# LN1 of a transformer trunk in groups of four channel tiles, with its element-wise work on VectorE

## The chip, the cores and the metric

The kernel runs on one core of one Trainium2 chip. The metric is the device time of one execution in microseconds (us). TensorE, VectorE, ScalarE, GpSimd and SyncE have an instruction queue each, in the fixed order in which the program was written; semaphores order them among each other. In the rows they are PE (PEld is its weight load), DVE, ACT, POOL and SP.

## The reference

One encoder layer works on 576 tokens of 2048 channels (512 of a prompt, 64 of a sample). The change lies between the mixer's last projection and the first product of the feed-forward network:

```python
x = layer_norm(DN_ALPHA * x + g1 * mix, ln1_g, ln1_b)      # mix = m @ w_out
u = ln_plain(x) * (1 + sc2) + sh2
f = (jax.nn.silu(u @ w_gate) * (u @ w_up)) @ w_down
x = layer_norm(DN_ALPHA * x + g2 * f, ln2_g, ln2_b)
```

Each normalization needs mean and variance over the 2048 channels of a token, and the second, parameter-free one (LN0) works on what the first (LN1) gives. Everything is fp32. The vectors sc2, sh2 and g1 differ between prompt and sample.

## The kernel before

Activations lie channel-major: 16 tiles of 128 channels (partitions) by 576 tokens. The tokens are worked in two halves, hf = 0 with 320 and hf = 1 with 256. An fp32 product is made of three matmuls: weights and activations are both split into a high and a low part (hi, lo and xh, xl), and each step of 128 input channels (a **tick**) does hi by xh, hi by xl and lo by xh (`mm_steps`, L312 to L316; in the last stage below, L1351). ScalarE makes hi of a weight block of 128 by 1024 (L215), VectorE makes lo (L220); a block serves 8 ticks. There are four pairs of hi and lo, so that the blocks of the next 24 ticks can be ready ahead of TensorE (`take`, `advance`).

The four stages that the prediction speaks of follow each other on TensorE:

- **A**: the projection with `w_out` for hf 0, 256 ticks of 320 columns. Beside it the other engines run the chain of LN1 and LN0 for hf 1.
- **B**: gate and up projection for hf 1, eight tiles of 32 ticks of 256 columns (`gate_up(ft, 1)`). Beside it runs the chain for hf 0.
- **C**: the same for hf 0, 256 ticks of 320 columns. Beside it `combo` makes sums and differences of the activation blocks, which the next stage multiplies.
- **D**: the first hidden tile (ft 8) of the rest of gate and up, which are done by seven products of 24 matmuls of 288 columns each, in the order 2, 4, 3, 5, 1, 6, 7. Products 6 and 7 read the differences SD and SE, which are made while the first five run.

What runs beside TensorE is set by the list `fill.bg`. At each tick the list earns a credit, `fill.rate`, and its first step is issued when the credit covers the step's cost; a step of kind "pe" waits until 16 ticks have passed since the last other step. Since every queue is in order, the list sets where a step stands between the weight splits.

The chain (`ln_chain`, L1050) has 18 steps for each of three passes, one tile of 128 channels by 320 or 256 tokens in a step:

- `center`: VectorE subtracts the mean (L1078), ScalarE squares (L1080), GpSimd adds the squares up (L1071). A matmul with a matrix of 1/2048 (L1061) sums over the partitions and spreads the result to all of them; `newton_rsqrt` (L334) makes rstd at full width, with Ln and Exp on ScalarE.
- `affine`: VectorE multiplies by gain and rstd (L1087), ScalarE adds the bias (L1090) and squares (L1091), GpSimd adds the squares up and VectorE the values (L1071).
- `modulate`: VectorE subtracts the mean (L1105) and multiplies by scale and rstd (L1107), ScalarE adds the shift and writes xh (L1112), VectorE makes xl (L1120), and ScalarE keeps the residual (L1114), which a DMA stores (L1117). While these steps head the list, GpSimd makes lo of the weight blocks (L219).

A `combo` has five steps for 4 tiles, 128 by 1152: a on GpSimd (L1187), b and c on VectorE (L1190, L1195, L1197), d on ScalarE (L1201), e on VectorE (L1205). For SE, b is on GpSimd too.

Of the kernel before, what the change touches and what calls it, by code (L numbers as in the profile page):

```python
# [14 lines left out]
P = 128  # L15
# [22 lines left out]
def tile_trunk(ctx, tc, x_prompt, x_sample, c_prompt, c_sample, cache_k, cache_v, state_pool,  # L38
# [43 lines left out]
    def f(ap):  # L82
        return ap.bitcast(F32)
# [59 lines left out]
    class Weights:  # L143
# [59 lines left out]
        def advance(self, late=False):  # L203
            if self.nu < len(self.units):
                i = self.nu
                self.nu += 1
                a, b, _ = self.units[i]
                raw = self.view(a) if b is None else self.sum_of.pop(i)
                if i in self.direct:
                    self.ready.append((raw, a))  # L210
                    return
                kk, n = raw.shape[1], raw.shape[1] * raw.shape[2]
                hi, lo = (split3(t[:, :n], kk) for t in self.pairs[self.np % len(self.pairs)])
                self.np += 1
                nc.scalar.activation(hi, raw, AF.Copy)  # L215
                self.combine(i + 1)

                def low():
                    eng = nc.gpsimd if fill.bg and fill.bg[0][0] == "mod" else self.engs[i % len(self.engs)]  # L219
                    (eng or nc.vector).tensor_tensor(lo, raw, f(hi), op=OP.subtract)  # L220
                    if b is None:
                        self.release(a)

                if late:
                    fill.at(3, low)
                else:
                    low()
                self.ready.append((hi, lo))
# [15 lines left out]
    class Fill:  # L244
# [779 lines left out]

    cv = Carve(misc)
    axb = [cv(640), cv(640)]
    cv.o = 1920
    SR = [cv(320), cv(256)]
    s1_t = cv(320)
    cv.o = 1280  # L1030
    nwt = [cv(320), cv(320)]
    lt = Carve(region("late", [P, 2048]))
    s2_t, rs_t, sqt = lt(320), lt(320), [lt(320), lt(320)] + nwt

    def load_ax(hf, j2):
        n = HS[hf]
# [10 lines left out]
    def res(hf, j):  # L1047
        return R0[:, j, :] if hf == 0 else R1[j // 8][:, j % 8, :]

    def ln_chain(hf):  # L1050
        n = HS[hf]
        cost = 0.6 if hf else 1.15
        s1, s2, rs = s1_t[:, 0:n], s2_t[:, 0:n], rs_t[:, 0:n]
        mean, var = AT[0][:, 0:n], AT[1][:, 0:n]
        nw = [t[:, 0:n] for t in nwt]
        steps = []

        def pe(*pairs):
            def go():
                for src, dst in pairs:  # L1060
                    nc.tensor.matmul(dst, ones, src, start=True, stop=True)  # L1061
            steps.append(("pe", 0, go))

        def st(cost, f, kind="v"):
            steps.append((kind, cost, f))

        def acc(eng, s, j, t):
            if j == 0:
                eng.tensor_copy(s, t)
            else:  # L1070
                eng.tensor_tensor(s, s, t, op=OP.add)  # L1071

        def sq(j):
            return sqt[j % 4][:, 0:n]

        def center(j):
            if j < 16:
                nc.vector.tensor_tensor(res(hf, j), res(hf, j), mean, op=OP.subtract)  # L1078
            if 0 <= j - 1 < 16:
                nc.scalar.activation(sq(j - 1), res(hf, j - 1), AF.Square)  # L1080
            if 0 <= j - 2:
                acc(nc.gpsimd, s2, j - 2, sq(j - 2))

        def affine(j):
            if j < 16:
                x = res(hf, j)
                nc.vector.scalar_tensor_tensor(x, x, vt2[:, 16 + j:17 + j], rs, op0=OP.mult, op1=OP.mult)  # L1087
            if 0 <= j - 1 < 16:
                x = res(hf, j - 1)
                nc.scalar.activation(x, x, AF.Identity, bias=vt2[:, 31 + j:32 + j])  # L1090
                nc.scalar.activation(sq(j - 1), x, AF.Square)  # L1091
            if 0 <= j - 2:
                acc(nc.gpsimd, s2, j - 2, sq(j - 2))
                acc(nc.vector, s1, j - 2, res(hf, j - 2))

        def rstd2():
            t = sqt[0][:, 0:n]
            nc.scalar.activation(t, mean, AF.Square)
            nc.vector.tensor_tensor(t, var, t, op=OP.subtract)
            newton_rsqrt(rs, t, n, nw)  # L1100

        def modulate(j):
            if j < 16:
                t = sq(j)
                nc.vector.tensor_tensor(t, res(hf, j), mean, op=OP.subtract)  # L1105
                for a, e, v in SEG[hf]:
                    nc.vector.scalar_tensor_tensor(t[:, a:e], t[:, a:e], modv("sc2", j, v), rs[:, a:e],  # L1107
                                                   op0=OP.mult, op1=OP.mult)
            if 0 <= j - 1 < 16:
                x = res(hf, j - 1)  # L1110
                for a, e, v in SEG[hf]:
                    nc.scalar.activation(xh(hf, j - 1)[:, a:e], sq(j - 1)[:, a:e], AF.Identity,  # L1112
                                         bias=modv("sh2", j - 1, v))
                nc.scalar.activation(x, x, AF.Identity, bias=mb[:, 1:2], scale=ALPHA)  # L1114
                if j % 4 == 0:
                    src = R0[:, j - 4:j, :] if hf == 0 else R1[(j - 4) // 8][:, (j - 4) % 8:(j - 4) % 8 + 4, :]
                    nc.gpsimd.dma_start(RESD[hf][:, j - 4:j, :], src)  # L1117
            if 0 <= j - 2:
                for a, e, v in SEG[hf]:
                    nc.vector.scalar_tensor_tensor(xl(hf, j - 2)[:, a:e], sq(j - 2)[:, a:e], modv("sh2", j - 2, v),  # L1120
                                                   f(xh(hf, j - 2)[:, a:e]), op0=OP.add, op1=OP.subtract)

        pe((SR[hf], mean))
        for j in range(18):
            st(cost, lambda j=j: center(j))
        pe((s2, var))
        st(2.0, lambda: newton_rsqrt(rs, var, n, nw))
        for j in range(18):
            st(cost, lambda j=j: affine(j))
        pe((s1, mean), (s2, var))  # L1130
        st(2.5, rstd2)
        for j in range(18):
            st(cost, lambda j=j: modulate(j), "mod")
        return steps

    for hf in (1, 0):
        n = HS[hf]
        for j in range(16):
# [5 lines left out]
            for jj in (j - 1, j):  # L1144
# [6 lines left out]
                if jj == 0:  # L1151
                    nc.vector.tensor_copy(SR[hf], x)
                else:
                    nc.vector.tensor_tensor(SR[hf], SR[hf], x, op=OP.add)
            nx = (1 - hf) * 8 + j // 2 + 2
            if nx < 16:
                load_ax(1 - nx // 8, nx % 8)
# [24 lines left out]
    def combo(x, y, op, dst, k, t, neg=False, eng=nc.vector):  # L1182

        t3 = split3(t[:, 0:1152], 4)

        def a():
            nc.gpsimd.tensor_tensor(t3, x(k, 4, 0)[0][2], y(k, 4, 0)[0][2], op=op)  # L1187

        def b():
            eng.tensor_tensor(t3, t3, f(x(k, 4, 1)[0][2]), op=OP.add)  # L1190

        def c():
            v = f(y(k, 4, 1)[0][2])
# [55 lines left out]
    for i, st in enumerate(todo):  # L1249
        a, b, c, d, e = st  # L1250
        if i == 0:
            chain.append((0.3, a))
        chain.append((1.2, b))
        if i:
            chain.append((1.2, todo[i - 1][4]))
            if i + 1 < len(todo):
                chain.append((0.3, todo[i + 1][0]))
            else:
                chain.append((0.3, SD[0][0]))
        elif len(todo) > 1:  # L1260
# [326 lines left out]
```

## Time and profile before

| | us |
|---|---|
| median of three runs (lowest, highest) | 3023.73 (3021.2, 3024.65) |
| the profiled execution | 3023.36 |
| its span, first to last instruction | 3021.6 |
| busy: PE, PEld | 2940.7 (97%), 2894.0 (96%) |
| busy: DVE, ACT, POOL | 2158.1 (71%), 1108.7 (37%), 494.1 (16%) |
| mean granted TensorE clock | 0.988 of full speed |

Busy time is the sum of an engine's instructions; the duration of an instruction is longer than its distance from the next where the two overlap. The page divides the span into 40 slices. TensorE's digit is 9 in 35 of them, 8 in the 1st, 18th and 22nd and 7 in the 20th and 40th; the granted clock is 7 tenths in the 20th, 8 in the 40th and 9 in the others. The 17th to the 22nd slice hold the four stages.

### The profile page before, as it was taken

What the parts mean: (1) busy time and instruction counts of PE and PEld (TensorE: products, weight loads), DVE (VectorE), ACT (ScalarE), POOL (GpSimd) and SP (SyncE); (2) the same over time, 40 slices, a digit from 0 to 9 for tenths busy, and PEclk for the clock granted to TensorE, in tenths of its full rate; (3) what the DMA queues carried; (4) which work ended last, traced back from release to release, by engine and by line L of the source; (5) the groups of instructions that cost most, each with busy time, mean ns of one, the idle gap of its engine ahead of it and who ended that gap; (6) DMA issues with size and microseconds to landing.
All of it is one profiled execution on the core that took longest, in us unless ns stands there. A gap on an engine that the chain in (4) does not pass through costs nothing. (4 is left out here: it accounts for less than half of the span.)

```text
span 3021.6 us, 52534 instructions
## 1 busy us (share of the span) xinstructions
PE 2940.7 (97%) x21675; PEld 2894.0 (96%) x21675; DVE 2158.1 (71%) x3310; ACT 1108.7 (37%) x1512; POOL 494.1 (16%) x504
## 2 busy tenths in 40 slices
PE   8999999999999999989798999999999999999997
PEld 7999999999999999989698999999999999999997
DVE  6777676898878757697887877777777753333467
ACT  4533333332222224465533434343433432122333
POOL 0023222113223220344432000000000010000001
PEclk9999999999999999999799999999999999999998
DMA  9864544675555446646453344343343473233444
GB/s 304 279 215 143 150 137 142 202 226 173 155 165 167 137 138 195 176 150 175 144 161 96 100 115 109 96 122 102 100 123 96 124 258 116 92 103 115 154 160 147
DMA packets 636015, 458.13 MB, mean 152 GB/s; under 512 B 17215, under 2 KB 619807, under 8 KB 634430
## 3 DMA queue, kind: packets, MB, share of 16 engines
q1 hardware_dynamic: 621136, 406.38, 45.7%
q0 software_dynamic: 14336, 48.24, 4.5%
q8 instruction: 169, 2.77, 0.4%
q14 instruction: 72, 0.59, 0.1%
q10 hardware_dynamic: 302, 0.15, 0.0%
HBM read 422.66 MB, written 32.04 MB: 150 GB/s over the span
## 5 line engine op out<-in xcount | busy, mean ns | idle before, releaser
L215 ACT ACTIVATE hi<-raw 128x1024 fp32r<-128x1024 f32 x689 | 724.5, 1057 | 1118.8 <-PE bank L314 341.9
L220 DVE TENSOR_TENSOR lo<-raw,hi 128x1024 fp32r<-128x1024 f32 x677 | 841.8, 1246 | 406.5 <-ACT hi L215 399.3
L316 PE MATMUL mm<-xh,lo 128*128 128x320 f32 (+1 forms) x2912 | 712.0, 297 | 23.4 <-DVE lo L220 13.3
L312 PE MATMUL mm<-xh,hi 128*128 128x320 f32 (+1 forms) x2912 | 727.7, 302 | 0.8 <-ACT hi L215 0.8
L314 PE MATMUL mm<-xl,hi 128*128 128x320 f32 (+1 forms) x2912 | 710.5, 296 | 7.9 <-DVE xl L1120 7.9
L316 PEld LDWEIGHTS mm<-xh,lo 128*128 128x128 f32 x2912 | 486.0, 190 | 27.0 <-DVE lo L220 15.8
L312 PEld LDWEIGHTS mm<-xh,hi 128*128 128x128 f32 x2912 | 490.1, 190 | 10.5 <-issue 4.0
L314 PEld LDWEIGHTS mm<-xl,hi 128*128 128x128 f32 x2912 | 486.9, 190 | 13.1 <-DVE xl L1120 12.6
L370 DVE SCALAR_TENSOR_TENSOR late<-raw,csil,late 128x256 f32<-128x256 f32 x960 | 418.7, 495 | 8.7 <-DMA raw<-in_w_ada_dram 8.6
L1351 PE MATMUL bank<-xh,hi 128*128 128x288 f32 x1152 | 341.3, 296 | 3.5 <-ACT xh L1201 3.5
L1351 PE MATMUL bank<-xl,hi 128*128 128x288 f32 x1152 | 341.2, 296 | 1.6 <-DVE xl L1205 1.6
L1351 PE MATMUL bank<-xh,lo 128*128 128x288 f32 x1152 | 341.0, 296 | 1.6 <-DVE lo L220 1.6
L312 PE MATMUL bank<-xh,hi 128*128 128x320 f32 (+1 forms) x1280 | 315.5, 295 | 2.2 <-DVE misc L1307 2.2
L316 PE MATMUL bank<-xh,lo 128*128 128x320 f32 (+1 forms) x1280 | 315.1, 295 | 1.6 <-DVE lo L220 1.6
L314 PE MATMUL bank<-xl,hi 128*128 128x320 f32 (+1 forms) x1280 | 314.4, 295 | 0.0
L1351 PEld LDWEIGHTS bank<-xh,hi 128*128 128x128 f32 x1152 | 216.8, 188 | 3.7 <-ACT xh L1201 3.7
L1351 PEld LDWEIGHTS bank<-xl,hi 128*128 128x128 f32 x1152 | 216.7, 188 | 2.2 <-DVE xl L1205 2.2
L1351 PEld LDWEIGHTS bank<-xh,lo 128*128 128x128 f32 x1152 | 216.8, 188 | 1.9 <-DVE lo L220 1.9
L312 PEld LDWEIGHTS bank<-xh,hi 128*128 128x128 f32 x1280 | 214.3, 188 | 2.5 <-DVE misc L1307 2.5
L316 PEld LDWEIGHTS bank<-xh,lo 128*128 128x128 f32 x1280 | 214.2, 188 | 1.8 <-DVE lo L220 1.8
L314 PEld LDWEIGHTS bank<-xl,hi 128*128 128x128 f32 x1280 | 213.4, 189 | 0.0
L375 POOL PARTITION_ALL_REDUCE late<-late x32 | 118.4, 3699 | 288.6 <-DVE late L370 244.2
(404 smaller groups left out, 4161.9 us busy)
## 6 DMA issues: line engine op xcount, KB each, us to landing
raw<-in_w_ada_dram SPq DMA_DIRECT2D x176, 512.0 KB, 4.8
raw<-in_w_in_dram SPq DMA_DIRECT2D x120, 512.0 KB, 4.4
raw<-in_w_down_dram SPq DMA_DIRECT2D x120, 512.0 KB, 3.3
raw<-in_w_gate_dram SPq DMA_DIRECT2D x104, 512.0 KB, 4.6
raw<-in_w_up_dram SPq DMA_DIRECT2D x104, 512.0 KB, 5.2
raw<-in_w_out_dram SPq DMA_DIRECT2D x64, 512.0 KB, 4.5
raw<-in_w_sb_out_dram SPq DMA_DIRECT2D x32, 512.0 KB, 4.7
hd<-misc POOLq DMA_DIRECT2D x36, 288.0 KB, 2.4
```

The costliest lines, as they stand in the source:

```text
L215: nc.scalar.activation(hi, raw, AF.Copy)
L220: (eng or nc.vector).tensor_tensor(lo, raw, f(hi), op=OP.subtract)
L312: nc.tensor.matmul(o, wh[:, k, cw], xh(xk + k), start=s and u not in join, stop=False)
L314: nc.tensor.matmul(o, wh[:, k, cw], xl(xk + k), start=False, stop=False)
L316: nc.tensor.matmul(o, wl[:, k, cw], xh(xk + k), start=False, stop=e and u not in hold)
L370: nc.vector.scalar_tensor_tensor(acc[:, v, :], raw[:, k, :], s, acc[:, v, :], op0=OP.mult, op1=OP.add)
L375: nc.gpsimd.partition_all_reduce(late["red"], late["acc"][grp % 2], P, bass_isa.ReduceOp.add)
L1351: nc.tensor.matmul(b[BANK[m]], n[w][:, k, :], SOP[m][x](k), start=not st and k == 0 and i == 0, stop=k == 7 and i == 2, skip_group_check=st)
```

## The change

- The chain works on four channel tiles at a time, 128 by 1280 (hf 0) or by 1024 (hf 1). VectorE does all subtractions, multiplications and additions, ScalarE squares, gain and bias, scale and shift, xh and the residual. A step issues its ScalarE part one step later than the VectorE part that feeds it. Each step's cost is given in ticks.
- rstd: a matmul with the squares as stationary operand gives the variance with tokens on partitions, one column per 128 tokens (`column`); VectorE adds EPS, GpSimd takes the power -0.5 of 2 or 3 columns (`rstd`), and a matmul with the identity spreads it to a row on all partitions (`spread`). Ln and Exp and the Newton step go.
- A "pe" step waits a number of ticks of its own: 12, 8 or 4.
- All of `combo` is on VectorE, and lo of a weight block always is. In ft 8 the list is emptied ahead of product 7, not 6.
- The sum of the values that LN1 starts from (`SR`) is made over two tiles at a time.

```diff
@@ Weights.advance
-                    eng = nc.gpsimd if fill.bg and fill.bg[0][0] == "mod" else self.engs[i % len(self.engs)]
-                    (eng or nc.vector).tensor_tensor(lo, raw, f(hi), op=OP.subtract)
+                    (self.engs[i % len(self.engs)] or nc.vector).tensor_tensor(lo, raw, f(hi), op=OP.subtract)
@@ Fill.step
-                    if self.n - self.last < 16:
+                    if self.n - self.last < cost:
@@ ln_chain
+        w = fill.rate if hf else 0.26
...
+        T4 = [split3(lnb[0][:, 1280 * i:1280 * i + 4 * n], 4) for i in range(4)]
+        s1, s2 = T4[2], T4[3]
+        mean, rs = AT[0][:, 0:n], AT[1][:, 0:n]
+        starts = (0, 128, n - 128)[:n // 128 + (n % 128 > 0)]
...
+        def column(c, s):
+            for t, a in enumerate(starts):
+                for i in range(2):
+                    nc.tensor.matmul(AT[2][:, c + t:c + t + 1], s[:, i, a:a + P], ones[:, 0:1], start=i == 0, stop=i == 1)
+
+        def spread():
+            for t, a in enumerate(starts):
+                o = 128 * t - a
+                nc.tensor.matmul(AT[1][:, a + o:a + P], stat[:, 8 + t:9 + t].to_broadcast([P, P]), ident[:, o:P],
+                                 start=True, stop=True)
...
+            nc.gpsimd.tensor_tensor(stat[:, 8:8 + nt], v, nhalf.to_broadcast([P, nt]), op=OP.pow)
...
+            steps.append(("v", min(ticks * w, 2.4), go))
...
+        def center(g):
+            tt(grp(g), grp(g), wide(mean), op=OP.subtract)
...
+        def add2(g, src):
+            tt(s2, T4[0] if g == 1 else s2, T4[src], op=OP.add)
...
+        def norm(g):
+            tt(grp(g), grp(g), wide(rs), op=OP.mult)
...
+        pe(12, (row, mean, SR[hf]))
+        st(5, (center, 0))
+        st(5, (center, 1), (sq, 0, True))
...
+        st(7, (add2, 3, 0), (fold, s2))
+        pe(12, (column, 0, s2))
+        st(4, (rstd, False))
+        pe(8, (spread,))
+        st(5, (norm, 0))
+        st(5, (norm, 1), (gain, 0, 0))
...
+        pe(12, (row, mean, s1), (column, 0, s2), (column, 4, s1))
+        st(4, (rstd, True))
+        st(3, (sub, 0))
+        st(3, (sub, 1))
+        pe(4, (spread,))
+        st(4, (modulate, 0))
+        st(4, (sub, 2), (shift, 0, 0))
...
+        st(4, (high, 3), (keep, 2))
+        st(3, (keep, 3))
+        st(3, (low, 3))
@@ combo
-            nc.gpsimd.tensor_tensor(t3, x(k, 4, 0)[0][2], y(k, 4, 0)[0][2], op=op)
+            nc.vector.tensor_tensor(t3, x(k, 4, 0)[0][2], y(k, 4, 0)[0][2], op=op)
...
-    SE = [combo(A12, A22, OP.subtract, A12, 4 * i, TMP[i], eng=nc.gpsimd) for i in range(2)]
+    SE = [combo(A12, A22, OP.subtract, A12, 4 * i, TMP[i]) for i in range(2)]
...
-            if (ft, m) == (8, 6):
+            if (ft, m) == (8, 7):
                 fill.flush_bg()
```

VectorE in stage B, first pass of the chain for hf 0 (L1110 center, L1116 sum of squares, L1107 fold, L1276 SwiGLU product, L219 lo; `at` is the mean in PSUM, `oc` holds the squares), after the change:

```order
L1110 TENSOR_TENSOR oa<-oa,at_74 128x1280
L219 TENSOR_TENSOR lo_70<-raw_65,hi_68 128x1024
L1110 TENSOR_TENSOR oa<-oa,at_74 128x1280 x2
L219 TENSOR_TENSOR lo_71<-raw_66,hi_69 128x1024
L1110 TENSOR_TENSOR oa<-oa,at_74 128x1280
L1276 TENSOR_TENSOR misc<-misc,mm_73 128x256
L1116 TENSOR_TENSOR oc<-oc 128x1280
L219 TENSOR_TENSOR lo_71<-raw_66,hi_69 128x1024
L1116 TENSOR_TENSOR oc<-oc 128x1280
L219 TENSOR_TENSOR lo_70<-raw_65,hi_68 128x1024
L1116 TENSOR_TENSOR oc<-oc 128x1280
L1107 TENSOR_TENSOR oc<-oc 128x640
```

Sixteen subtractions of 320 columns have become four of 1280, and the sum of squares, which stood on GpSimd, is now between the weight splits.

GpSimd in the same stage, before (L1071 sums of squares, L1217 stores of the hidden tile; part of the first pass):

```order
L1071 TENSOR_TENSOR late<-late,misc 128x320 x2
L1071 TENSOR_TENSOR late<-late 128x320 x2
L1071 TENSOR_TENSOR late<-late,misc 128x320 x2
L1071 TENSOR_TENSOR late<-late 128x320
L1217 DMA hd<-misc 128x256
L1071 TENSOR_TENSOR late<-late 128x320
L1071 TENSOR_TENSOR late<-late,misc 128x320 x2
```

and after the change, the whole stage (L1098 the power, L1148 the residual's stores):

```order
L1277 DMA hd<-misc 128x256
L1098 TENSOR_TENSOR small<-small 128x3
L1277 DMA hd<-misc 128x256 x3
L1098 TENSOR_TENSOR small<-small 128x3
L1277 DMA hd<-misc 128x256
L1148 DMA resd_81<-oa 128x1280 x2
L1277 DMA hd<-misc 128x256
L1148 DMA resd_81<-oa 128x1280 x2
L1277 DMA hd<-misc 128x256 x2
```

Only two powers of three columns and the DMA issues are left there.

VectorE in stage D, from SD's second xl to SE's (L1265 is e, L1247 a, L1250 b, L1257 c, L198 sums of weight blocks, L1348 the sum behind product 4), after the change:

```order
L1265 TENSOR_TENSOR xl<-misc,xh 128x4x288
L198 TENSOR_TENSOR raw_67<-raw_65,raw_66 128x1024
L1247 TENSOR_TENSOR late<-xh 128x1152
L219 TENSOR_TENSOR lo_70<-raw_67,hi_68 128x1024
L1247 TENSOR_TENSOR misc<-xh 128x1152
L1250 TENSOR_TENSOR late<-late,xl 128x1152
L198 TENSOR_TENSOR raw_67<-raw_65,raw_66 128x1024
L1348 TENSOR_TENSOR misc<-bank_14896,misc 128x288
L1250 TENSOR_TENSOR misc<-misc,xl 128x1152
L219 TENSOR_TENSOR lo_70<-raw_67,hi_68 128x1024
L1257 TENSOR_TENSOR late<-late,xl 128x1152
L1257 TENSOR_TENSOR misc<-misc,xl 128x1152
```

The four rows of L1247 and L1250 stood on GpSimd; after these twelve come L219, L198, L1353, L219 and the two L1265 of SE.

## Rows read from the trace of the kernel before

**Rows 1.** Windows, stages A to D and undisturbed: length, busy PE PEld DVE ACT POOL, PEclk, DMA.

```profile
1231.40:1365.10 133.70, 121.47 (x779) 119.69 (x778) 113.25 (x198) 72.88 (x135) 56.51 (x50) 0.95 0.52 154
1365.10:1470.40 105.30, 98.35 (x778) 95.61 (x777) 83.49 (x107) 65.67 (x101) 50.90 (x42) 0.95 0.57 166
1470.40:1611.60 141.20, 125.75 (x770) 119.14 (x768) 112.03 (x104) 56.98 (x76) 41.05 (x23) 0.90 0.48 148
1611.60:1646.40 34.80, 25.43 (x170) 23.97 (x169) 30.89 (x21) 12.61 (x16) 14.93 (x5) 0.95 0.24 66
1800.00:1900.00 100.00, 100.00 (x750) 100.00 (x749) 78.31 (x90) 39.77 (x53) 2.70 (x5) 1.00 0.37 102
```

**Rows 2.** Timeline of PE at the stages' borders: start, duration, instruction, [idle before].

```profile
1231.40 0.31 PE L312 MATMUL mm<-xh,hi 128*128 128x320 f32 x1
...
1365.06 0.28 PE L312 MATMUL mm<-xh,hi 128*128 128x256 f32 x1
...
1470.40 0.31 PE L312 MATMUL mm<-xh,hi 128*128 128x320 f32 x1
...
1612.85 0.53 PE L1351 MATMUL bank<-ob,hi 128*128 128x288 f32 x2 [1.05 <-DVE misc L1216]
...
1646.41 0.43 PE L1351 MATMUL bank<-ob,hi 128*128 128x288 f32 x2
...
1668.87 0.43 PE L1351 MATMUL bank<-ob,hi 128*128 128x288 f32 x2
```

**Rows 3.** Timeline of DVE: its reads of finished tiles in undisturbed stretches.

```profile
1220.29 0.61 DVE L1149 SCALAR_TENSOR_TENSOR ob<-mm,mods,misc 128x192 f32<-128x192 f32 x2 [0.63 <-PE mm L316]
...
1231.60 0.61 DVE L1149 SCALAR_TENSOR_TENSOR ob<-mm,mods,misc 128x192 f32<-128x192 f32 x2 [0.63 <-PE mm L316]
...
1246.10 0.55 DVE L1149 SCALAR_TENSOR_TENSOR oa<-mm,mods,misc 128x320 f32<-128x320 f32 x1 [0.64 <-PE mm L316]
...
1260.18 0.55 DVE L1149 SCALAR_TENSOR_TENSOR oa<-mm,mods,misc 128x320 f32<-128x320 f32 x1 [1.02 <-PE mm L316]
```

**Rows 4.** Waits of PE in the whole span: total, times, longest.

```profile
PE mm L316 <- DVE lo L220: 13.3, 11, 2.4
PE mm L316 <- POOL lo L220: 10.2, 4, 4.4
PE mm L314 <- DVE xl L1120: 7.9, 12, 2.6
```

**Rows 5.** Timeline of DVE at the start of stage D.

```profile
1614.31 1.36 DVE L1205 TENSOR_TENSOR xl<-late,xh 128x1152 fp32r<-128x1152 f32 x1 [0.38 <-ACT xh L1201]
1615.59 1.22 DVE L220 TENSOR_TENSOR lo<-raw,hi 128x1024 fp32r<-128x1024 f32 x1
1616.72 3.84 DVE L1205 TENSOR_TENSOR xl<-misc,xh 128x1152 fp32r<-128x1152 f32 x1
1620.48 3.70 DVE L198 TENSOR_TENSOR raw<-raw,raw 128x1024 f32<-128x1024 f32 x1
```

**Rows 6.** Timeline of POOL in the same stretch.

```profile
1615.76 3.59 POOL L1187 TENSOR_TENSOR late<-xh 128x1152 f32<-128x1152 f32 x1 [2.12 <-DVE xl L1205]
1619.42 3.67 POOL L1190 TENSOR_TENSOR late<-late,xl 128x1152 f32<-128x1152 f32 x1
```

**Rows 7.** Timeline of PE: two matmuls of one column, between products (stage of the mixer).

```profile
658.86 0.35 PE L953 MATMUL at<-small,to 128*128 128x1 f32 x2 [0.64 <-DVE small L952]
```

**Rows 8.** Timeline of PE in stage D, at product 7.

```profile
1639.58 0.40 PE L1351 MATMUL bank<-xh,hi 128*128 128x288 f32 x1 [3.45 <-ACT xh L1201]
1640.97 0.61 PE L1351 MATMUL bank<-xl,hi 128*128 128x288 f32 x1 [0.99 <-DVE xl L1205]
1641.38 0.44 PE L1351 MATMUL bank<-xh,lo 128*128 128x288 f32 x1
1641.62 0.44 PE L1351 MATMUL bank<-xh,hi 128*128 128x288 f32 x1
```

**Rows 9.** A group of ACT with bias and scale from tiles: count, busy, mean ns, idle.

```profile
L1472 ACT ACTIVATE oa<-oa,misc 128x512 f32<-128x512 f32 x4 | 2.9, 802 | 0.6 <-DVE misc L1464 0.6
```

More of the change, by code (lines that the diff above doesn't have):

```diff
@@ L1048, in res, with rows @@
         return R0[:, j, :] if hf == 0 else R1[j // 8][:, j % 8, :]
+    def rows(hf, j, k):
+        return R0[:, j:j + k, :] if hf == 0 else R1[j // 8][:, j % 8:j % 8 + k, :]
     def ln_chain(hf):
         n = HS[hf]
[L1052 to L1055, printed above, removed]
-        steps = []
-        def pe(*pairs):
-            def go():
-                for src, dst in pairs:
-                    nc.tensor.matmul(dst, ones, src, start=True, stop=True)
-            steps.append(("pe", 0, go))
@@ L1064, in st @@
[L1064 to L1069, printed above, removed]
-            else:
[L1071 to L1094, printed above, removed]
@@ L1123, in ln_chain @@
[L1123 to L1133, printed above, removed]
+        w = fill.rate if hf else 0.26
+        if not lnb:
+            lnb.append(region("oc", [P, 5120]))
@@ new lines, in ln_chain, with wide, grp, pe @@
+        T4 = [split3(lnb[0][:, 1280 * i:1280 * i + 4 * n], 4) for i in range(4)]
+        s1, s2 = T4[2], T4[3]
+        mean, rs = AT[0][:, 0:n], AT[1][:, 0:n]
+        starts = (0, 128, n - 128)[:n // 128 + (n % 128 > 0)]
+        nt = len(starts)
+        tt = nc.vector.tensor_tensor
+        steps = []
+        def wide(t):
+            return t[:, None, :].to_broadcast([P, 4, n])
+        def grp(g):
+            return rows(hf, 4 * g, 4)
+        def pe(gate, *fns):
+            def go():
+                for fn, *a in fns:
+                    fn(*a)
+            steps.append(("pe", gate, go))
@@ new lines, in row @@
+        def row(dst, s):
+            for i in range(2):
+                nc.tensor.matmul(dst, ones, s[:, i, :], start=i == 0, stop=i == 1)
+        def column(c, s):
+            for t, a in enumerate(starts):
+                for i in range(2):
+                    nc.tensor.matmul(AT[2][:, c + t:c + t + 1], s[:, i, a:a + P], ones[:, 0:1], start=i == 0, stop=i == 1)
[4 more added lines that the diff above has]
+                                 start=True, stop=True)
@@ new lines, in st, with go, fold, sq @@
+        def st(ticks, *fns):
+            def go():
+                for fn, *a in fns:
+                    fn(*a)
+            steps.append(("v", min(ticks * w, 2.4), go))
+        def fold(s):
+            tt(s[:, 0:2], s[:, 0:2], s[:, 2:4], op=OP.add)
+        def center(g):
+            tt(grp(g), grp(g), wide(mean), op=OP.subtract)
+        def sq(g, first=False):
+            nc.scalar.activation(T4[g if first and g < 3 else g % 2 if not first else 0], grp(g), AF.Square)
+        def add2(g, src):
+            tt(s2, T4[0] if g == 1 else s2, T4[src], op=OP.add)
@@ new lines, in add1, with gain, sub @@
+        def add1(g):
+            tt(s1, grp(0) if g == 1 else s1, grp(g), op=OP.add)
+        def norm(g):
+            tt(grp(g), grp(g), wide(rs), op=OP.mult)
+        def gain(g, i):
+            for j in range(4 * g + 2 * i, 4 * g + 2 * i + 2):
+                nc.scalar.activation(res(hf, j), res(hf, j), AF.Identity, bias=vt2[:, 32 + j:33 + j],
+                                     scale=vt2[:, 16 + j:17 + j])
+        def sub(g):
+            tt(T4[g], grp(g), wide(mean), op=OP.subtract)
@@ new lines, in ln_chain @@
+        st(5, (add1, 2), (gain, 3, 1), (sq, 2))
+        st(5, (add2, 2, 0), (sq, 3))
+        st(7, (add1, 3), (fold, s1))
+        st(7, (add2, 3, 1), (fold, s2))
+        pe(12, (row, mean, s1), (column, 0, s2), (column, 4, s1))
[5 more added lines that the diff above has]
+        st(4, (sub, 2), (shift, 0, 0))
+        st(4, (modulate, 1), (shift, 0, 1))
+        st(4, (sub, 3), (high, 0))
+        st(4, (modulate, 2), (shift, 1, 0))
```

107 lines of the change are left out of this document (54 added, 53 removed).

## The prediction

> **What bounds the kernel now.** I read the page first: TensorE is busy for 97% of the span, so time can come only from where TensorE waits or runs at the lower clock. The windows by stage [rows 1] show where that is: in an undisturbed stretch TensorE is busy for 100 of 100 us at a granted clock of 1.00; in A to D it is idle for 12.2, 7.0, 15.5 and 9.4 us, and the clock is 0.90 to 0.95.
>
> Waits and clock are priced together by the pace. Undisturbed, 96 matmuls take 11.31 us at 256 columns (1220.29 to 1231.60) and 14.08 us at 320 (1246.10 to 1260.18) [rows 3], and one hidden tile of 168 matmuls at 288 columns takes 22.46 us (1646.41 to 1668.87) [rows 2]. Stages A, B and C are eight times 96 matmuls each. From the borders [rows 2], with C ending at 1612.85 - 1.05 = 1611.80:
>
> - A: 133.7 us for 112.6, 21.0 lost;
> - B: 105.3 for 90.5, 14.9 lost;
> - C: 141.4 for 112.6, 28.8 lost;
> - D: 34.6 for 22.5, 12.1 lost.
>
> Together 76.8 us. That is the most this change can give; the rest of the span it leaves as it is.
>
> TensorE waits for lo of a weight block, made on VectorE or on GpSimd, and for xl of the chain's last pass [rows 4]. VectorE is late because its instructions are stretched. At the start of D [rows 5] an instruction of 1152 columns takes 1.36 us and one of 1024 takes 1.22; then two take 3.84 and 3.70. GpSimd [rows 6] works from 1615.76 to 1619.35; the VectorE instruction that began at 1616.72 ends 1.21 us after that, at 1620.56. GpSimd's next ends at 1623.09, and VectorE's next 1.09 us after it. So a VectorE instruction that meets one of GpSimd waits for its end and then takes its usual time. GpSimd has 56.5, 50.9, 41.1 and 14.9 us of work in A to D, and 2.7 in 100 us undisturbed [rows 1].
>
> **The change, part by part.** What GpSimd did goes to VectorE, in wide instructions. Their price is the distance between starts, since neighbours overlap: 1.28 us for 1152 columns (1614.31 to 1615.59) and 1.13 for 1024 (1615.59 to 1616.72) [rows 5]. So 128 columns cost 0.15, 1280 cost 1.43, 640 about 0.7 and 512 about 0.55. None of 1280 columns is in the trace: below 1.28 it can't be, and at twice 1.43 it is a rival below.
>
> *A.* The chain for hf 1 has 29 instructions of 1024 columns (four each of center, norm, sub, modulate and low, three each of the three sums) and three folds of 512: 34.4 us. The 32 weight splits cost 36.2, 16 reads of finished tiles at 0.55 [rows 3] and seven wide sums of SR at 0.7 cost 13.7. Together 84 us under 112.6. At the densest place a wide instruction comes every 4 ticks, that is 4 x 14.08 / 32 = 1.76 us, beside half a split, 1.13 + 0.57 = 1.70. VectorE keeps up, and what stays is TensorE's own: 12 matmuls of one column, 4 for rows, 4 to spread. Two of one column take 0.35 us [rows 7]; at 0.18 each, 20 cost 3.6, of which four stood there before. I take 3.
>
> *B.* A tick is 11.31 / 32 = 0.353 us, and here VectorE is tight. The order puts 46 ticks (16.2 us) between the mean and the first `column`. VectorE must do 7 wide instructions (10.0), a fold (0.7), 5.75 splits (6.5) and 1.4 SwiGLU products at most 0.55 each (0.8): 18.0, so TensorE stands for 1.8 us. Between the first spread and the second mean lie 71 ticks (25.1 us) against 10 wide (14.3), two folds (1.4), 8.9 splits (10.0) and 2.2 products (1.2): 26.9, again 1.8. In the last pass no matmul waits for the chain itself, only for splits that stand behind it, and three blocks are ready ahead (24 ticks, 8.5 us); a pile of VectorE of some 4 us is under that. I give it 1. The chain's own 28 matmuls cost up to 28 x 0.18 = 5.0; I take 4, since four stood there before. After a wait the clock falls: at product 7 matmuls of 288 columns come every 0.24 us (1641.38 to 1641.62) [rows 8] against 22.46 / 168 = 0.134, which is the lower level of 1.2 GHz. The waits here are half as long as those in front of that row, so I add 1.5. Sum 10.
>
> *C.* The last xl of the chain stands over 32 ticks (11.3 us) before the end of B on VectorE's queue, so the waits for xl, nearly all at the start of C, go. A combo instruction comes every 6 ticks (2.64 us) and costs 1.28, with 0.85 of splits beside it. Left: 1.
>
> *D.* From the first xl of SD, at 1614.31 [rows 5], VectorE has eight instructions of 1152 columns (10.2), eight of 1024 (9.0) and two sums of at most 0.55 [rows 3] (1.1) until it begins SE's first xl: 1634.6, and 1636.0 at its end. TensorE starts D at 1612.85 [rows 2], and six products of 22.46 / 7 = 3.21 bring it to product 7 at 1632.1. It waits 3.9 us there, where it now begins at 1639.58 and waits again until 1640.97 [rows 8]. With 2 for the clock ft 8 ends 5.9 us later than undisturbed, and the 1.05 in front of D stays: 6.9 left.
>
> Sum: 3 + 10 + 1 + 6.9 = 20.9 left of 76.8, a gain of 55.9. The profiled execution took 3023.36 us, 0.4 under the median; so 3023.4 - 55.9 = 2967.5, and I say **2967 us**. Its bounds: with no wait in B and only TensorE's own matmuls left, A 2, B 4, C 0, D 5 is 11, or 2958. The far ends are the rivals'.
>
> ScalarE carries more too: per half 16 gains, 16 scales and shifts with both factors from tiles, each under the 0.80 us that 512 columns take [rows 9]. It is idle for 39.6 us of 105.3 in B today [rows 1] and has the same three blocks of lead.
>
> One rule speaks against this shape. In the rows the engine in question is 79% busy in B (83.5 of 105.3) and still makes TensorE wait. The Trainium skill (Perfetto Trace Analysis, Optimizing Scalar/DVE Operations) says that where Vector is not saturated but leaves bubbles on other engines, instructions should be broken up; by it the wide form costs, and the next case would be the result. No run here shows it yet.
>
> **The rivals.**
>
> *Wide steps hand over too late, 2986 us.* In a pass ScalarE and VectorE alternate: six sums of squares, three sums of values and four xl of a half wait for a wide ScalarE instruction, 13 hand-overs. If VectorE stands at each for about 1.2 us, that is 15.6 us a half. In A it is under the 28 us that VectorE has free, and costs perhaps 3; in B, where 46 and 71 ticks are already overfull, it adds 11; in C and D 2 each at the combos' d. Left: 6 + 21 + 3 + 9 = 39, gain 38. For it: B has no room. Against it: the step's delay of 5 ticks (1.8 us) is longer than one such instruction.
>
> *Wide VectorE instructions are slow of themselves, 3060 us.* Then the 3.7 us of rows 5 belong to width, and 1280 columns take 2.86. VectorE has 118 us in A under 112.6, and in the chain's own ticks some 21 too many; in B 46 too many; D gains 10 us of work. With half as much again for the clock in A and a fifth in B: 34 + 60 + 5 + 17 = 116 left, 39 more than now. Between 1.43 (20 left) and 2.86 (116) the sign turns at 76.8, near 1.6 times, 2.3 us. Against it: the same 1152 columns took 1.36 without GpSimd. The Trainium skill (SBUF — State Buffer, Who interferes with whom) says that a VectorE instruction with two SBUF inputs and a GpSimd one that reads SBUF exclude each other for the whole instruction; the rows agree (3.84 beside 3.59).
>
> *The change doesn't do what it says:* GpSimd would still be beside VectorE, or the chain would be flushed at the end of B. The order shows neither, only 3-column powers and DMA issues; what is left is that the waits come from something the rows don't show, and the time stays.
>
> **How the numbers follow.** The forecast has a chance of 0.68, late hand-overs 0.20, slow wide instructions 0.07, no change 0.05. A difference under 0.2%, 6 us, can't be told from none here. The forecast and its near bound reach from 2958 to about 2978; 8 times in 10 the range must take in most of the late hand-overs, to 2992, and a little under the near bound: **2953 to 2992**. Faster 0.89 (the first two cases and a part of the last), same 0.04, slower 0.07.
>
> **What would show it.** Right: instructions of 1280 columns on VectorE at about 1.5 us (duration), no lo above 1.3 us, a GpSimd nearly idle, A in 116 us, B in 100, C in 114, D in 29, and the waits of TensorE at `column`, at the second mean and at product 7. The forecast is wrong if VectorE's wide instructions take 2 us or more, if TensorE waits in B for lo or spread by over 6 us in all, or if the granted clock in A to C stays under 0.97.

## The result, and the profile after

The changed kernel takes 2974.6 us (median of 4 runs, 2971.8 to 2978.5), the kernel before, beside it, 3024.2: a ratio of 0.984, 95% interval 0.983 to 0.985. It is faster by 49.6 us; the forecast was a gain of 55.9 and 2967 us, with 2953 to 2992 as the range. The profiled execution took 2972.9 us with a span of 2971.2.

The four stages with the borders of the changed kernel, answering to [rows 1] (windows; the columns are as there):

```profile
1231.25:1349.20 117.95, 117.95 (x810) 117.74 (x809) 86.98 (x94) 68.96 (x96) 9.17 (x13) 1.00 0.64 182
1349.20:1456.23 107.03, 102.90 (x826) 101.32 (x825) 84.38 (x78) 71.74 (x88) 7.78 (x13) 0.95 0.60 183
1456.23:1569.03 112.80, 112.80 (x770) 112.55 (x768) 83.30 (x74) 43.45 (x48) 4.33 (x8) 1.00 0.54 160
1569.03:1597.60 28.57, 24.33 (x170) 24.09 (x169) 27.65 (x28) 13.19 (x16) 0.54 (x1) 0.94 0.29 80
```

Against the same undisturbed lengths as in the prediction (112.6, 90.5, 112.6, 22.5) A now loses 5.3 us, B 16.5, C 0.2 and D 6.1: 28.1 in place of 76.8. C gained 28.6, A 15.7, D 6.0, and B nothing at all: it loses 16.5 now and lost 14.9 before.

What TensorE waits for in these stages, answering to [rows 4] (waits; in total, times, longest):

```profile
PE bank L1401 <- DVE xl L1265: 3.2, 1, 3.2
PE at L1081 <- DVE oc L1107: 2.9, 2, 2.0
PE bank L1401 <- DVE misc L1276: 1.0, 1, 1.0
PE at L1076 <- DVE oc L1107: 0.7, 1, 0.7
PE mm L315 <- DVE lo L219: 0.5, 1, 0.5
```

L1107 is the fold, L1081 `column`, L1076 `row`; the first line is product 7 of D. The waits for xl at C's start and for GpSimd's lo are gone. VectorE's groups from 1231 to 1490 us, that is in A, B and the start of C (groups by form; busy, mean ns, idle time before them), show what the wide instructions cost:

```profile
L219 DVE TENSOR_TENSOR lo<-raw,hi 128x1024 fp32r<-128x1024 f32 x74 | 89.9, 1220 | 34.5 <-ACT hi L215 34.3
L1116 DVE TENSOR_TENSOR oc<-oc 128x1280 f32<-128x1280 f32 x6 | 8.9, 1483 | 0.0
L1122 DVE TENSOR_TENSOR oa<-oa,at 128x1280 f32<-128x1280 f32 x4 | 5.8, 1480 | 0.0
L1119 DVE TENSOR_TENSOR oc<-oc,oa 128x1280 f32<-128x1280 f32 x2 | 3.0, 1482 | 0.0
L1151 DVE TENSOR_TENSOR xl<-oc,xh 128x1280 fp32r<-128x1280 f32 x4 | 5.9, 1482 | 0.0
```

1280 columns take 1.48 us, as forecast from the spacing of smaller ones, so the rival "Wide VectorE instructions are slow of themselves" (2.3 us and more) falls at once. L1116, L1119 and L1151 are the sums of squares, the sums of values and xl, the 13 places of a half where VectorE takes over from ScalarE; VectorE stood 0.0 us in front of them, so the rival "Wide steps hand over too late" falls by these rows as well.

B's loss lies mostly in one place, the chain's second reduction for hf 0. TensorE's own rows there (timeline; start, duration, idle time before it and what ended it), and the windows around them:

```profile
1402.94 1.34 PE L1076 MATMUL at<-oc,to 128*128 128x320 f32 x4 [0.72 <-DVE oc L1107]
1406.33 5.28 PE L1081 MATMUL at<-to,oc 128*128 128x1 f32 x24 [2.05 <-DVE oc L1107]
```

```profile
1405.00:1410.00 5.00, 3.67 (x18) 3.67 (x18) 3.85 (x5) 0.00 (x0) 0.54 (x1) 0.60 0.62 187
1410.00:1415.00 5.00, 5.00 (x24) 5.00 (x25) 3.17 (x6) 0.15 (x1) 0.86 (x1) 0.50 0.55 154
1415.00:1420.00 5.00, 5.00 (x41) 5.00 (x40) 3.10 (x4) 1.88 (x3) 0.00 (x0) 0.88 0.32 93
```

The granted clock fell to 0.50 at 1406.0 us, while TensorE waited and before the first of the 24 records, and stayed there for 10 us. The code issues 12 matmuls of one column there and the trace has 24 records: one fp32 matmul is two records. So [rows 7] showed one matmul, not two, and the prediction's price of TensorE's own work in the chain rests on a row that was misread; what it came to is worked out further down.

### The profile page after: what moved, and what is told of

It is laid out like the page before. It is cut to its first block, busy times and chain, and to the rows that moved or that the text cites. A ratio compares the mean times of both kernels' runs of the same rounds, so it can differ in the third digit from the quotient of the medians.

```text
span 2971.2 us, 52217 instructions
## 1 busy us (share of the span) xinstructions
PE 2925.0 (98%) x21755; PEld 2888.7 (97%) x21755; DVE 2100.5 (71%) x3144; ACT 1097.0 (37%) x1432; POOL 355.6 (12%) x420
## 5 line engine op out<-in xcount | busy, mean ns | idle before, releaser
L219 DVE TENSOR_TENSOR lo<-raw,hi 128x1024 fp32r<-128x1024 f32 x689 | 844.1, 1227 | 429.9 <-ACT hi L215 422.7
L311 PE MATMUL mm<-xh,hi 128*128 128x320 f32 (+1 forms) x2912 | 720.4, 300 | 0.0
L315 PE MATMUL mm<-xh,lo 128*128 128x320 f32 (+1 forms) x2912 | 703.6, 294 | 1.1 <-DVE lo L219 1.1
L313 PE MATMUL mm<-xl,hi 128*128 128x320 f32 (+1 forms) x2912 | 702.6, 294 | 0.0
L311 PEld LDWEIGHTS mm<-xh,hi 128*128 128x128 f32 x2912 | 484.1, 188 | 8.5 <-issue 3.8
```

Of the source, the lines that this page charges most:

```text
L219: (self.engs[i % len(self.engs)] or nc.vector).tensor_tensor(lo, raw, f(hi), op=OP.subtract)
L311: nc.tensor.matmul(o, wh[:, k, cw], xh(xk + k), start=s and u not in join, stop=False)
L313: nc.tensor.matmul(o, wh[:, k, cw], xl(xk + k), start=False, stop=False)
L315: nc.tensor.matmul(o, wl[:, k, cw], xh(xk + k), start=False, stop=e and u not in hold)
```

## Which half of the change gives what

Theory 1 was that GpSimd working beside VectorE cost the time, wherever it stood. The first two runs split the change.

**Combos alone**, on the kernel before; the new order of the combos' steps goes with these lines:

```diff
-            nc.gpsimd.tensor_tensor(t3, x(k, 4, 0)[0][2], y(k, 4, 0)[0][2], op=op)
+            nc.vector.tensor_tensor(t3, x(k, 4, 0)[0][2], y(k, 4, 0)[0][2], op=op)
...
-            if (ft, m) == (8, 6):
+            if (ft, m) == (8, 7):
```

> The kernel before with only the second half of the change: the combos' a and b on VectorE, their new order, and the queue emptied in front of product 7. The two LayerNorm chains stay as before. Theory 1 (GpSimd beside VectorE is what cost the time, wherever it stood): D loses 6.1 us in place of 12.1, and in C the waits after 1530 us go, where 4.7 us were lost between 1530 and 1570; the waits for xl at the start of C stay. A gain of 10 to 11 us, 3013 to 3014 us. Rival (the combos only suffered from the chain's late end): no gain over 3 us, 3021 to 3025 us.

Measured: 3011.6 us against 3024.9 (ratio 0.996, 0.994 to 0.997), 1.4 us under the expected range.

**Chain alone** is the changed kernel with these parts as before:

> The changed kernel with the combos of before: a, and two of the b, on GpSimd again, in the order of before, emptied in front of product 6. The chains stay as changed. Theory 1 (the two halves add up): D loses 12 us again and C some 5, so the gain is about 38 of 49 us, 2983 to 2986 us. Rival (the chain's end was all of it): as the changed kernel, 2972 to 2977 us.

Measured: 2990.4 us (0.989, 0.987 to 0.990), 4 us above the expected range. The two gains, 13.3 and 34.5, make 47.8 of 49.6. Stage C, from its first matmul of 320 columns to the 1.05 us wait ahead of D, shows how they add (windows, first the combos alone, then the chain alone):

```profile
1474.00:1606.40 132.40, 122.76 (x770) 117.42 (x768) 105.96 (x112) 57.76 (x76) 13.35 (x15) 0.91 0.52 158
```

```profile
1457.80:1579.60 121.80, 116.53 (x770) 113.99 (x768) 90.24 (x67) 42.65 (x48) 29.97 (x16) 0.99 0.51 149
```

C took 141.4 before. The combos take 9.0 off, the chain 19.6, and 141.4 - 28.6 is the 112.8 of the changed kernel. My expectation for the combos was too low in C (4.7): I had counted only the stretch after 1530 us. D's 6.0 us come with the combos alone. That run changes the combos' engine, their order and the point where the list is emptied at once; no run separates these, so for the combos GpSimd as the cause isn't shown. The windows of C speak for it: with the combos partly on GpSimd (chain alone) VectorE's 67 instructions take 90.2 us, without it 74 take 83.3.

## Is it GpSimd, and what of it

Both runs put one GpSimd instruction into every VectorE step of the changed chain; nobody waits for it.

```diff
+                nc.gpsimd.tensor_tensor(lt[:, 1024:1536], lt[:, 0:512], lt[:, 512:1024], op=OP.add)
```

> The changed kernel, where each of the chain's 33 VectorE steps per half also issues one GpSimd addition of two 512-column tiles into a third that nobody reads (so GpSimd has about 1.45 us of work per step, some 48 us in A and in B each, as it had before). No instruction waits for it. Theory 1 (a GpSimd instruction that reads two tiles holds VectorE's up): VectorE's 1280-column instructions rise from 1.48 us to 2.2 us or more in the mean, B loses 25 us or more beyond its 16.5, and the kernel takes 3000 to 3030 us. Rival (the gain came from fewer and wider instructions, and GpSimd beside them costs nothing): 1.48 us stays, 2971 to 2979 us.

```diff
+                nc.gpsimd.memset(lt[:, 0:2048], 1.0)
```

> The same place and number, but each GpSimd instruction only fills a 2048-column tile with a constant: it reads nothing. Theory 1, by which it is GpSimd's reading that excludes VectorE: 1280-column instructions stay at 1.48 to 1.55 us and the time at 2971 to 2980 us. Rival (whatever GpSimd does holds VectorE up): as with the additions, 1280 columns at over 2 us and 3000 us or more.

Measured: 3000.7 us with the additions, 2976.0 with the constants. (There are 38 steps a half, not 33.) The two pieces of work are nearly alike: 76 instructions, 138.7 and 138.3 us of GpSimd. A and B, taken from their first matmuls, last 123.3 and 127.0 with the additions; with the constants 117.9 and 107.1, as without. The groups with the additions (1231 to 1490 us again):

```profile
L1103 POOL TENSOR_TENSOR late<-late 128x512 f32<-128x512 f32 x76 | 138.7, 1825 | 4.6
...
L219 DVE TENSOR_TENSOR lo<-raw,hi 128x1024 fp32r<-128x1024 f32 x66 | 119.0, 1813 | 15.0 <-ACT hi L215 14.8
L1118 DVE TENSOR_TENSOR oc<-oc 128x1280 f32<-128x1280 f32 x6 | 13.2, 2207 | 0.0
L1153 DVE TENSOR_TENSOR xl<-oc,xh 128x1280 fp32r<-128x1280 f32 x4 | 9.2, 2298 | 0.0
L1135 DVE TENSOR_TENSOR oc<-oc,at 128x1280 f32<-128x1280 f32 x4 | 5.9, 1479 | 0.6 <-PE at L1087 0.6
L1124 DVE TENSOR_TENSOR oa<-oa,at 128x1280 f32<-128x1280 f32 x4 | 5.8, 1478 | 0.0
```

and with the constants:

```profile
L1103 POOL MEMSET late<- 128x2048 f32 x76 | 138.3, 1819 | 3.1
...
L219 DVE TENSOR_TENSOR lo<-raw,hi 128x1024 fp32r<-128x1024 f32 x74 | 90.0, 1222 | 37.8 <-ACT hi L215 37.5
L1118 DVE TENSOR_TENSOR oc<-oc 128x1280 f32<-128x1280 f32 x6 | 8.9, 1484 | 0.0
```

Reading is what costs, and not every VectorE instruction pays. Those whose inputs are both SBUF tiles (sums of squares L1118, xl L1153, lo L219) rise by half in the mean; those with one input in PSUM (`at`: norm L1124, modulate L1135) keep 1.48 us. A stretch of B with the additions shows both kinds beside a GpSimd that works without a break (timelines of GpSimd, then VectorE):

```profile
1390.68 10.79 POOL L1103 TENSOR_TENSOR late<-late 128x512 f32<-128x512 f32 x6
```

```profile
1392.99 2.87 DVE L1124 TENSOR_TENSOR oa<-oa,at 128x1280 f32<-128x1280 f32 x2
1395.79 2.27 DVE L219 TENSOR_TENSOR lo<-raw,hi 128x1024 fp32r<-128x1024 f32 x1
```

Two instructions of 1280 columns take 2.87 us together there, as they do undisturbed, and a split takes 2.27 in place of 1.22. The Trainium skill (SBUF — State Buffer, Who interferes with whom) says just this: a VectorE instruction with two SBUF inputs contends with a GpSimd one that reads SBUF, not with one that only writes, and one with at most one SBUF input, outside the 2-port modes, doesn't contend. The trace agrees in all three points (2.21 us, 1.48, 1.48). The rows alone also give a likely reason why my expectation for B was somewhat high: B lost 20 us more, not 25, and 16 of the 29 wide instructions of a half read mean or rstd from PSUM.

So theory 1 holds for the chain: GpSimd's additions bring 26 us back, the constants 1.4, which is within the spread of the runs. The 26 aren't a measured share of the chain's 34.5. The additions keep GpSimd busy for 138.7 us in A and B, where all of its work before was 107.4 [rows 1]; and TensorE's waits for GpSimd's own splits, 10.2 us in [rows 4], can't return with instructions that nobody waits for.

**Width.** The same kernel, every grouped instruction issued as single tiles:

```diff
-        tt = nc.vector.tensor_tensor
+        def tt(o, x, y, op):
...
+            for i in range(o.shape[1]):
+                nc.vector.tensor_tensor(o[:, i, :], x[:, i, :], y[:, i, :], op=op)
```

> The changed kernel with every grouped VectorE instruction of the chain issued as single tiles (four of 320 or 256 columns in place of one of 1280 or 1024), at the same places; GpSimd stays out. Theory 1 (keeping GpSimd's reads away made the gain): four of 320 at about 0.45 us are 0.3 to 0.4 us more than the 1.43 of one wide; ten wide steps in each of B's two tight legs make that 3 to 4 us a leg, A has room for it: 2976 to 2984 us. Rival (fewer, wider instructions made the gain): most of the 49 us goes, 3000 us or more. Second rival (wide steps hand over late, narrow ones sooner): faster than the changed kernel, under 2971 us.

Measured: 2979.3 us (0.986, 0.984 to 0.987), as theory 1 has it. B lasts 110.2 against 107.0, A 117.9 as before.

```profile
L1066 DVE TENSOR_TENSOR oa<-oa,at 128x320 f32<-128x320 f32 x32 | 13.2, 481 | 0.7 <-PE at L1082 0.7
L1066 DVE TENSOR_TENSOR oc<-oc 128x320 f32<-128x320 f32 x30 | 12.6, 483 | 0.0
```

Four of 0.48 us make 1.93 against 1.48. Width is worth 3 us, in B alone, and breaking VectorE's instructions up gained nothing. ScalarE's squares and xh stay four tiles wide in this run, so it says little about the hand-overs between the two engines; VectorE's idle times above do. The Trainium skill (Perfetto Trace Analysis, Optimizing Scalar/DVE Operations), weighed in the prediction, says that breaking up instructions may let work be completed sooner where Vector isn't saturated but causes bubbles on other engines. In this run it did not (2979.3 against 2974.6 us).

## What is left in B

Theory 2: at the second reduction TensorE waits for the fold, its clock falls, and its own matmuls and the products behind them run at the lower level.

```diff
-        pe(12, (row, mean, s1), (column, 0, s2), (column, 4, s1))
+        pe(12 if hf else 22, (row, mean, s1), (column, 0, s2), (column, 4, s1))
```

> The changed kernel with the second reduction of the chain for hf 0 (in B) issued 22 ticks after the fold in place of 12. Theory 2 (TensorE waits there for the fold, the clock falls because it waited, and the chain's 26 matmuls and the products behind them then run at the lower clock): the waits of 0.7 and 2.0 us go, L1081's 24 records take 3 us in place of 5.3, B loses some 9 in place of 16.5, and the kernel takes 2966 to 2969 us. Rival (the clock falls because of the matmuls of one column themselves): only the wait goes, the clock of 0.50 stays for 10 us, 2971 to 2973 us. Second rival (B is full, the wait moves behind it): no gain, 2973 us or more.

Measured: 2968.9 us (0.982, 0.981 to 0.983); B lasts 100.7 in place of 107.0. The size is as theory 2 said, but the rival's clock shows as well (timeline, then windows):

```profile
1406.83 1.24 PE L1076 MATMUL at<-oc,to 128*128 128x320 f32 x4
1407.90 2.93 PE L1081 MATMUL at<-to,oc 128*128 128x1 f32 x24
```

```profile
1408.00:1410.00 2.00, 2.00 (x21) 2.00 (x19) 2.00 (x3) 0.00 (x0) 0.54 (x1) 1.00 0.32 106
1410.00:1411.00 1.00, 1.00 (x7) 1.00 (x7) 1.00 (x2) 0.00 (x0) 0.00 (x0) 0.65 0.76 206
1411.00:1412.00 1.00, 1.00 (x6) 1.00 (x6) 0.83 (x6) 0.00 (x0) 0.00 (x0) 0.50 1.12 327
```

No wait stands in front, and still the clock goes to 0.50 (1.2 GHz) at the end of the 24 records, for some 3.5 us in place of 10. So it fell in two ways: in the changed kernel during the wait and before the columns, here without a wait, at the end of a row of matmuls of one column.

**Half as many matmuls**, by folding once more on VectorE:

```diff
             tt(s[:, 0:2], s[:, 0:2], s[:, 2:4], op=OP.add)
+            tt(s[:, 0], s[:, 0], s[:, 1], op=OP.add)
```

> The changed kernel where each fold adds once more (n columns on VectorE, 0.4 us, four times per pair of halves), so that the second mean, and all columns, take one matmul in place of two. By the records of the changed kernel (24 of one column 3 us at full clock, a second mean of two matmuls 1.0 to 1.3 us): A falls by 2 us, B by 2.8 at full clock and by some 4 where the clock is low, if TensorE's own matmuls are what is left in A: 2967 to 2970 us. Rival (they only fill time in which TensorE would wait anyway, and the later fold makes the wait longer): 2973 to 2977 us.

Measured: 2974.1 us, no gain to speak of. A falls by 1.8 (117.95 to 116.16), as expected; B only from 107.0 to 106.4, since the waits for the fold grew from 2.9 and 0.7 us to

```profile
PE at L1081 <- DVE oc L1108: 4.5, 2, 3.1
...
PE at L1077 <- DVE oc L1108: 1.3, 1, 1.3
```

The clock also fell a second time: it was 0.50 from 1373 to 1376 us, behind a wait of 1.4 us at the first columns. The rival was right in B.

**The mean first, the columns later**, with that fold:

```diff
-        pe(12, (row, mean, s1), (column, 0, s2), (column, 4, s1))
+        pe(10, (row, mean, s1), (column, 4, s1))
+        st(4, (sub, 0))
+        st(3, (sub, 1))
+        pe(8, (column, 0, s2))
         st(4, (rstd, True))
-        st(3, (sub, 0))
-        st(3, (sub, 1))
-        pe(4, (spread,))
+        pe(10, (spread,))
```

> The same extra fold, and in the second reduction the mean and the columns of the sum of values first, then the first two subtractions of the mean on VectorE, and the columns of the sum of squares 15 ticks and more behind its fold. Theory 2: both gains together, A loses 3.3 in place of 5.3, B about 6 in place of 16.5, the clock in B stays above 0.98: 2960 to 2964 us. Rival (either is hidden by the other): not under 2967 us.

Measured: 2973.0 us: a miss, and the time is the rival's. A lasts 116.2, B 103.8. The columns waited no more at the second reduction, but the mean did (2.0 us) and then the spread, for the rstd:

```profile
PE at L1086 <- POOL small L1098: 2.9, 1, 2.9
PE at L1077 <- DVE oc L1108: 2.0, 1, 2.0
```

**All of it later**, for hf 0:

```diff
-        pe(12, (column, 0, s2))
+        pe(12 if hf else 16, (column, 0, s2))
...
-        pe(10, (row, mean, s1), (column, 4, s1))
+        pe(10 if hf else 16, (row, mean, s1), (column, 4, s1))
         st(4, (sub, 0))
-        st(3, (sub, 1))
         pe(8, (column, 0, s2))
         st(4, (rstd, True))
-        pe(10, (spread,))
+        st(3, (sub, 1))
+        pe(8 if hf else 12, (spread,))
```

> As early_mean_fold1, but for hf 0 every matmul of the chain comes later behind the VectorE work it needs: first columns 16 ticks behind the fold (12 before), second mean 16 (10), rstd in front of the second subtraction, and the second spread 12 ticks behind that. Theory 2 in its final form (in B it is the waits for the chain, and a row of 24 records of one column, that let the clock fall; six records at a time do not): no wait at L1077, L1081 and L1086 above 0.5 us, granted clock 1.00 from 1356 us to the end of B, B loses its own matmuls alone, 5 to 6 us in place of 16.5, A 3.5 in place of 5.3: 2960 to 2964 us. Rival (the later chain ends too late for C): a wait for xl at C's start, 2968 us or more.

Measured: 2968.6 us (0.981, 0.980 to 0.983). TensorE waits nowhere in front of the chain's own matmuls, and the clock is 1.00 past the reduction, as expected; but B still lasts 101.1. The time is the rival's, but TensorE waits for no xl at C's start, so neither theory had the cause: a pile on ScalarE at the end of the last pass (timeline of ScalarE, then of TensorE).

```profile
1437.20 1.27 ACT L1145 ACTIVATE xh<-oc 128x1280 fp32r<-128x1280 f32 x1
1438.38 2.60 ACT L1148 ACTIVATE oa<-oa,small 128x1280 f32<-128x1280 f32 x2
1440.89 0.36 ACT L1277 ACTIVATE misc<-mm 128x256 f32<-128x256 f32 x1
1441.15 3.88 ACT L215 ACTIVATE hi<-raw 128x1024 fp32r<-128x1024 f32 x4
```

```profile
1442.24 0.38 PE L311 MATMUL mm<-xh,hi 128*128 128x256 f32 x1 [0.98 <-ACT hi L215]
1444.29 0.58 PE L315 MATMUL mm<-xh,lo 128*128 128x256 f32 x1 [1.54 <-DVE lo L219]
```

Four splits stand behind two scalings (`keep`, L1148) that nothing in B or C needs soon. So, **`keep` behind the pass**:

```diff
-        st(4, (keep, 0), (shift, 2, 0))
+        st(4, (shift, 2, 0))
...
-        st(4, (high, 3), (keep, 2))
-        st(3, (keep, 3))
-        st(3, (low, 3))
+        st(4, (high, 3))
+        st(4, (keep, 0))
+        st(4, (low, 3))
+        st(5, (keep, 1))
+        st(5, (keep, 2))
+        st(5, (keep, 3))
```

> As late_gates, with ScalarE's four scalings of x by ALPHA in each half taken from between the last pass's steps and put behind them. In late_gates ScalarE worked without a break from 1417 to 1445 us, two such scalings (2.60 us) stood in front of four weight splits, and TensorE waited 2.5 us for hi and lo and had a granted clock of 0.77 from 1440 to 1455. Theory 2: that wait was ScalarE's pile and nothing else, so it goes, the clock in B is 1.00 throughout and B loses some 6 us: 2962 to 2966 us. Rival (the last pass is too dense for ScalarE with or without them): the wait stays, 2967 to 2971 us.

Measured: 2962.5 us (0.980, 0.978 to 0.981). Its interval lies below the changed kernel's: this version beats both. Its stages A to C:

```profile
1231.70:1347.85 116.15, 116.15 (x796) 115.99 (x795) 88.24 (x97) 69.16 (x96) 8.35 (x13) 1.00 0.63 184
1347.85:1443.69 95.84, 95.09 (x806) 94.24 (x805) 85.36 (x81) 71.37 (x87) 7.20 (x12) 1.00 0.62 182
1443.69:1556.50 112.81, 112.81 (x770) 112.54 (x768) 83.54 (x75) 43.88 (x49) 4.87 (x9) 1.00 0.58 178
```

B loses 5.3 us in place of 16.5, A 3.6 in place of 5.3, and the clock is 1.00 in all three. VectorE is as busy in B as in the changed kernel (85.4 us against 84.4): it was not full, only asked at the wrong moment. This version folds once more, places the chain's matmuls later and moves `keep`; the last step is `keep`'s alone, as `late_gates` has all the rest (B 101.1 there, 95.8 here).

## The rstd in columns

Theory 3: columns and spread cost TensorE more than rows would. The edit takes the row form of before:

```diff
-        pe(12, (column, 0, s2))
+        pe(12, (row, AT[1][:, 0:n], s2))
         st(4, (rstd, False))
-        pe(8, (spread,))
...
-        pe(12, (row, mean, s1), (column, 0, s2), (column, 4, s1))
+        pe(12, (row, mean, s1), (row, AT[1][:, 0:n], s2))
```

> The changed kernel without its third part: variance and second mean stay rows, and rstd is made as before, over whole rows, by ScalarE's Ln and Exp and VectorE's Newton step, into SBUF; no columns, no spread. Theory 3 (the rstd in columns costs TensorE more than it gives): by the changed kernel's records columns and spread take 6.1 us in B and 4.0 in A at full clock, rows in their place 2.5 and 2.0; with the low clock of the second reduction that is 2 us less in A and 5 to 7 in B: 2966 to 2970 us. Rival (the row form holds up VectorE: it stood 3.5 us for ScalarE's table load, Ln and Exp at 1408.9 us in the kernel before, four times per pair of halves, and lo waits behind it): 2977 to 2985 us.

> As row_rstd, with the second reduction for hf 0 22 ticks behind the fold in place of 12. Theory 3: a further 1 to 3 us, the waits for the fold, 2964 to 2968 us. Rival (VectorE's stand is what counts, and the gate does not touch it): as row_rstd.

Measured: 2976.2 and 2974.1 us (0.984, 0.983 to 0.985; 0.983, 0.982 to 0.985); the first is the changed kernel's own time, so theory 3 misses, and its rival by 1 us. A is 1.9 us shorter (116.1), so rows are indeed the cheaper there; B isn't (107.7), because what TensorE saves it waits for: 4.2 us for the fold, 3.9 for lo and 0.9 for hi, where the changed kernel waits 4.1 in all. With the later gate, as its rival had it, the wait only moves to lo (waits of `row_gate22`):

```profile
PE mm L315 <- DVE lo L219: 7.3, 7, 1.5
...
PE at L1076 <- DVE oc L1095: 0.8, 1, 0.8
```

Where the column form with that gate waits 0.4 us for lo and reaches 2968.9, the row form waits 7.3: VectorE has more to do in B there (88.3 us against 84.2) and stands twice for 1.0 us for ScalarE's Ln and Exp. So the third part of the change is worth nothing as it was written, and perhaps 5 us once the reduction is late enough (the two intervals touch, 0.981 to 0.983 and 0.982 to 0.985, so this difference is likely and not certain).

## Why the prediction was right

The time lay in the range and the forecast's case came in: VectorE's instructions weren't stretched any more, and A, C and D came within 2.3 us each of what was forecast for them. The sum of what is left was 28.1, not 20.9; B alone is 6.5 over. By its steps:

- **GpSimd beside VectorE** as the cause: right for the chain, shown by the additions against the constants; argued for the combos.
- **1280 columns at 1.43 us apart, about 1.5 long**: right (1.48).
- **C, 1 us left**: 0.2. **D, 6.9**: 6.1, with a wait of 3.2 at product 7 where 3.9 was forecast.
- **A, 3 us**: 5.3. The term of TensorE's own matmuls was mis-sized. From start to start they take 4.8 us: twelve columns 2.5, four matmuls for rows 1.5, four to spread 0.7. So 0.18 each was right to spread, low for a column (0.21) and half of what a row takes (0.38). Besides, the four "which stood there before" should not have been taken off, since the loss is counted against lengths that hold none of them. Taking seven of A's matmuls away gave 1.8 us.
- **B, 10 us**: 16.5, the step that failed. Its waits were right in the sum: 4.6 forecast (1.8 + 1.8 + 1), 4.1 measured (0.8 in front of the first columns, 2.8 at the second reduction, 0.5 for lo). TensorE's own matmuls were forecast at 4 and take 7.2 at full clock, from start to start (the first row 0.84, the first columns 1.36, the spreads 0.59 and 0.58, and the second row with its columns 3.86 in `gate22`). The rest, 16.5 - 4.1 - 7.2 = 5.2, goes to the clock, for which I had 1.5: it stood at 0.50 for 10 us.
- **B's gain**: the working took the loss of B from 14.9 to 10. It rose by 1.6. My reading is that the price and the clock of the chain's matmuls took back what GpSimd's leaving gave; what the runs show is that 11 us of it go with later placing, one more fold and `keep` behind the pass (107.0 to 95.8).
- **"No lo above 1.3 us, GpSimd nearly idle"**: right (at most 1.23; 9.2 and 7.8 us in A and B). The sign "the granted clock in A to C stays under 0.97" came in for B (0.95) and not for A and C (1.00).

Of the rivals, slow wide instructions and late hand-overs fell by the profile, and no change by the result.

Open: D still loses 6 to 7 us, of which 3.2 is VectorE's last xl, and it wasn't tried to start that combo earlier. The seven products of D and of the hidden tiles behind it (first to last start of their matmuls of hi by xh) took 801.4 to 803.7 us in runs that don't differ there, so 2 us between single runs mean nothing.

## What to carry to other kernels

When GpSimd and VectorE work side by side, look at where the inputs lie: what two SBUF inputs on VectorE pay beside a reading GpSimd, an input in PSUM or a GpSimd that only writes doesn't. A reduction through TensorE is issued late enough that its input is surely there, since the wait can cost twice: itself (2.8 us here) and the clock behind it (some 5). After each repair read the waits again: here fold, spread and ScalarE's pile each hid the next.

## What the runs showed of the hardware

- An fp32 matmul has two records in the trace (12 issued, 24 records) and costs 0.21 us even with one column: in A of the changed kernel 16 records take 1.70 us from their first start to that of the next matmul, at a granted clock of 1.00.
- The granted clock fell to 0.50 at the end of 24 records of one column without any wait (`gate22`), and not behind 16 in A of the changed kernel (1.84 us) nor behind 6 in `late_gates`, each in one execution.
- The length of a wait alone didn't tell whether the clock fell. In `early_mean_fold1` it stayed at 1.00 behind waits of 1.4 and 2.0 us and fell to 0.50 behind one of 2.9; in `fold1` it fell behind the same 1.4 us at the first columns.
- GpSimd additions of 512 columns (1.82 us in the mean) beside VectorE lengthen a 1280-column instruction with two SBUF inputs from 1.48 to 2.21 us in the mean and leave one with a PSUM input at 1.48.
